# Two maps' query and key features side by side on the partitions, and their scores as pairs of 64-row products

## The chip, the cores and the metric

The kernel runs on one core of one Trainium2 chip. The metric is the device time of one execution in microseconds (us); three executions of the kernel before are shown, and their median is the time before.

## The reference

Two layers of a trunk over 512 latent tokens and 256 context tokens of width 1024. Each layer has a token-mixing part (a convolution branch and a differential attention, merged by gates) and an MLP. Only the attention is touched. It has 8 heads; each head has two softmax maps, and each map has its own queries and keys of 64 features:

```python
qb = q.reshape(B, nb, Q_BLOCK, N_HEADS, 2, QK_DIM).transpose(1, 0, 2, 3, 4, 5)
...
s = jnp.einsum('bqhcd,bkhcd->bhcqk', qi, keys, preferred_element_type=jnp.float32) * scale
p = jax.nn.softmax(s, axis=-1)
w = p[:, :, 0] - lam * p[:, :, 1]
return jnp.einsum('bhqk,bkhv->bqhv', w.astype(vals.dtype), vals)
```

Queries and keys are RMS-normalized over their 64 features, and those of latent tokens are rotated (rotary embedding) by cosine and sine tables. Latent queries read all 768 keys, context queries the 256 context keys. In the second layer only latent tokens have queries.

## The kernel before, in words

All values are float32. TensorE products run on float32r operands, and to keep the accuracy each operand is split into a high part (the value rounded to float32r, written by ScalarE) and a low part (the remainder, by VectorE or GpSimd). A full product takes three matmuls: high by high, high by low, low by high (`mm3`, lines 103 to 106).

Tokens lie in 6 tiles of 128 (tiles 0 to 3 latent, 4 and 5 context). Per layer, a loop over the heads `h` attends head `h` (`attend`) and, as filler between its steps, projects the next head (`qk_head`) and the next values (`v_pair`). `merge` deals the steps out by rough costs in us. That is only the order in which the program is written. The Tile framework's own scheduler then orders each engine's instructions by a simulated timeline, so that matmuls of several steps stand mixed on TensorE, and a product whose buffer comes free later is put later. The chip follows that order on each engine.

For head `h` and token tile `t`:

- `project(t)` makes queries and keys of both maps (tile `qk`, 128 tokens x 256), squares and sums them, and GpSimd takes the power -1/2 (L500). L501 multiplies. For latent tiles GpSimd makes the two rotary products `ra` and `rb` (L509, L513). Their sum is written twice into the tile `dup`, [128, 4, 2, 64], once by GpSimd and once by VectorE (L518), so that every 64 features stand twice side by side. Context tiles get the two copies by two GpSimd multiplications (L521).
- `turn(t, d)` turns `dup` by four TensorE transposes of 128x128 (L532, tile `qkT`, group 0 and 1 the queries of map 0 and 1, 2 and 3 the keys), so the features lie on the partitions, and each 64 features lie there twice, on partitions 0 to 63 and 64 to 127. ScalarE copies 128x512 to `QH` (L536), VectorE writes the queries' low parts `QL` (L537), and over the upper half of the keys their low parts (L539). So `QH[:, 2 + m]` holds the key's high part on 64 partitions and its low part on the other 64.
- `scores(t)` makes for each map `m` a PSUM tile `S` (pool `pS`, two buffers) of 128 queries x 768 keys, in a piece of 512 and one of 256 keys. One matmul over all 128 rows gives high query by high and low key at once (L660), a second adds the low query (L662). VectorE takes the row maximum of `S` (L664), ScalarE the exponential (L667), and that frees the buffer.
- The weights `e` are combined and turned (L690, tile `wT`), multiplied by the values (`av`), and normalized.

In the second layer the context tokens have keys only: `ctx_keys`, `ctx_norm` and `ctx_turn` project them, turn them, and turn them again in the doubled layout (L575, L579, L580).

The modulation of the next layer is computed beside the MLP by `ada_slab` (tile `adaps`): its matmuls (L216) have 32 columns of weights and address one of four column parts of the array by `tile_position=(0, 32 * j)`.

Of the kernel before, what the change touches and what calls it, by code (L numbers as in the profile page):

```python
# [8 lines left out]
F32 = mybir.dt.float32  # L9
F32R = mybir.dt.float32r  # L10
AF = mybir.ActivationFunctionType
# [3 lines left out]
P = 128  # L15
# [31 lines left out]
def f32(ap):  # L47
    return ap.bitcast(F32)
# [3 lines left out]
def trunk_kernel(  # L52
# [334 lines left out]
    for i in range(DEPTH):  # L387
# [90 lines left out]
        def qk_head(h):  # L478

            pre = first.pop("ps") if h == 0 else []  # L480
            w = first.pop("w") if h == 0 else qk_slab(i, h, both)
            QA = qp.tile([P, 4 * NT + 2 * nv], F32R, tag="qk", name=f"qk{i}_{h}")
            QH = QA[:, : 4 * NT].rearrange("p (g d) -> p g d", g=4)
            QL = QA[:, 4 * NT :].rearrange("p (g d) -> p g d", g=2)
            R = ap.tile([P, NTT, 4], F32, tag="rqk", name=f"rqk{i}_{h}")
            QKt[h] = QH, QL

            def project(t):
                given = t < len(pre)
                ps = pre[t] if given else mm_tile(f"qk{i}_{h}_{t}")  # L490
                for k in range(0 if given else KT):
                    mm3(ps[:, :256], hst(k, t), (w[0][:, k], w[1][:, k]), k == 0, k == KT - 1)
                rw = ap.tile([P, 4, QK], F32, tag="rw", name=f"rw{i}_{h}_{t}", bufs=4)
                nc.scalar.activation(out=rw, in_=ps[:, :256].rearrange("p (g d) -> p g d", g=4),
                                     func=AF.Copy)
                sq = sqs[next(turns) % 2]
                nc.scalar.activation(out=sq[:, :, :QK], in_=rw, func=AF.Square)
                r = R[:, t]
                nc.vector.tensor_reduce(out=r, in_=sq, axis=AX.X, op=ALU.add)
                nc.gpsimd.tensor_tensor(out=r, in0=r, in1=mhalf[:, :4], op=ALU.pow)  # L500
                (nc.gpsimd if last or t > 3 else nc.vector).tensor_tensor(  # L501
                    out=rw, in0=rw, in1=r.unsqueeze(2).to_broadcast([P, 4, QK]), op=ALU.mult)
                d = ap.tile([P, 4, 2, QK], F32, tag="dup", name=f"dup{i}_{h}_{t}", bufs=3)
                if t < 4:
                    a = ap.tile([P, 4, QK], F32, tag="sc", name=f"ra{i}_{h}_{t}", bufs=4)
                    b = ap.tile([P, 4, QK], F32, tag="sc", name=f"rb{i}_{h}_{t}", bufs=4)
                    v4 = rw.rearrange("p (s m) d -> p s m d", s=2)
                    bv = b.rearrange("p (s m) d -> p s m d", s=2)
                    nc.gpsimd.tensor_tensor(  # L509
                        out=a.rearrange("p (s m) d -> p s m d", s=2), in0=v4,  # L510
                        in1=L["tC"][:, t].unsqueeze(2).to_broadcast([P, 2, 2, QK]), op=ALU.mult)
                    for lo, o in ((0, hq), (hq, 0)):
                        nc.gpsimd.tensor_tensor(  # L513
                            out=bv[:, :, :, lo : lo + hq], in0=v4[:, :, :, o : o + hq],
                            in1=L["tS"][:, t, :, lo : lo + hq].unsqueeze(2)
                            .to_broadcast([P, 2, 2, hq]), op=ALU.mult)
                    for dup, eng in enumerate((nc.gpsimd, nc.vector)):
                        eng.tensor_tensor(out=d[:, :, dup], in0=a, in1=b, op=ALU.add)  # L518
                else:
                    for s in range(2):  # L520
                        nc.gpsimd.tensor_tensor(  # L521
                            out=d[:, 2 * s : 2 * s + 2],
                            in0=rw[:, 2 * s : 2 * s + 2].unsqueeze(2).to_broadcast([P, 2, 2, QK]),
                            in1=L["gr"][:, s].unsqueeze(1).unsqueeze(1)
                            .to_broadcast([P, 2, 2, QK]), op=ALU.mult)
                return d

            def turn(t, d):
                nm = f"qkT{i}_{h}_{t}"
                tp = turn_tile(nm) if turn_tile else mm_tile(nm)  # L530
                for g in range(4):
                    nc.tensor.transpose(tp[:, g * P : g * P + P],  # L532
                                        d[:, g].rearrange("p a d -> p (a d)"), ident)
                tpv = tp.rearrange("p (g d) -> p g d", g=4)
                ts = slice(t * P, t * P + P)
                nc.scalar.activation(out=QH[:, :, ts], in_=tpv, func=AF.Copy)  # L536
                nc.vector.tensor_tensor(out=QL[:, :, ts], in0=tpv[:, 0:2],  # L537
                                        in1=f32(QH[:, 0:2, ts]), op=ALU.subtract)
                nc.vector.tensor_tensor(out=QH[QK:, 2:4, ts], in0=tpv[QK:, 2:4],  # L539
                                        in1=f32(QH[QK:, 2:4, ts]), op=ALU.subtract)  # L540

            def ctx_keys():

# [7 lines left out]
            def ctx_norm(kc):  # L551
                tp = mm_tile(f"kcT{i}_{h}")
                for j in range(2):
                    nc.tensor.transpose(tp[:, j * P : j * P + P], kc[:, j * P : j * P + P], ident)
                rw = ap.tile([P, 4, QK], F32, tag="rw", name=f"rwc{i}_{h}", bufs=4)
                nc.scalar.activation(out=rw, in_=tp[:, :256].rearrange("p (g d) -> p g d", g=4),
                                     func=AF.Copy)
                sq = sqs[next(turns) % 2]
                nc.scalar.activation(out=sq[:, :, :QK], in_=rw, func=AF.Square)
                r = R[:, 4]  # L560
                nc.vector.tensor_reduce(out=r, in_=sq, axis=AX.X, op=ALU.add)
                nc.gpsimd.tensor_tensor(out=r, in0=r, in1=mhalf[:, :4], op=ALU.pow)
                nc.vector.tensor_tensor(out=rw, in0=rw, in1=r.unsqueeze(2).to_broadcast([P, 4, QK]),
                                        op=ALU.mult)
                d = ap.tile([P, 4, 2, QK], F32, tag="dup", name=f"dupc{i}_{h}", bufs=3)
                nc.gpsimd.tensor_tensor(
                    out=d, in0=rw.unsqueeze(2).to_broadcast([P, 4, 2, QK]),
                    in1=L["gr"][:, 1].unsqueeze(1).unsqueeze(1).to_broadcast([P, 4, 2, QK]),
                    op=ALU.mult)
                return d  # L570

            def ctx_turn(d):
                tp = mm_tile(f"kcD{i}_{h}")
                for g in range(4):
                    nc.tensor.transpose(tp[:, g * P : g * P + P],  # L575
                                        d[:, g].rearrange("p a d -> p (a d)"), ident)
                tpv = tp.rearrange("p (j m d) -> p m j d", j=2, m=2)
                o = QH[:, 2:4, CTXS].rearrange("p m (j d) -> p m j d", j=2)
                nc.scalar.activation(out=o, in_=tpv, func=AF.Copy)  # L579
                nc.vector.tensor_tensor(out=o[QK:], in0=tpv[QK:], in1=f32(o[QK:]),  # L580
                                        op=ALU.subtract)

            done = []
            for t in range(qt_n):
# [46 lines left out]
        def attend(h):  # L631
# [5 lines left out]
            def scores(t):  # L637
# [12 lines left out]
                ts = slice(t * P, t * P + P)  # L650
                es = []
                st = ap.tile([P, 8], F32, tag="st", name=f"st{nm}", bufs=4)
                for m in range(2):
                    S = pS.tile([P, 768], F32, tag="S", name=f"S{nm}_{m}")
                    for lo, hi in ((0, 512), (512, 768)):
                        lo = max(lo, kb * P)
                        if hi <= lo:
                            continue
                        o = slice(lo - kb * P, hi - kb * P)
                        nc.tensor.matmul(S[:, o], QH[:, m, ts], QH[:, 2 + m, lo:hi],  # L660
                                         start=True, stop=False)
                        nc.tensor.matmul(S[:, o], QL[:, m, ts], QH[:, 2 + m, lo:hi],  # L662
                                         start=False, stop=True)
                    nc.vector.tensor_reduce(out=st[:, m : m + 1], in_=S[:, :nkey], axis=AX.X,  # L664
                                            op=ALU.max, negate=True)
                    e = ap.tile([P, 768], F32, tag=f"e{m}", name=f"e{m}{nm}", bufs=2 - m)
                    nc.scalar.activation(out=e[:, :nkey], in_=S[:, :nkey], func=AF.Exp,  # L667
                                         bias=st[:, m : m + 1],
                                         accum_out=st[:, 2 + m : 3 + m])
                    es.append(e)  # L670
# [631 lines left out]
```

## Time and profile before

| | us |
|---|---|
| median of 3 executions | 2394.25 |
| lowest, highest | 2392.32, 2401.45 |
| the profiled execution | 2399.05 |
| its span in the trace | 2397.3 |
| TensorE busy with matmuls in it | 2317.9 (97%) |
| VectorE, ScalarE, GpSimd busy | 1349.1, 928.7, 679.7 |

In the rows of a profile, PE is TensorE's matmuls, PEld its weight loads, DVE VectorE, ACT ScalarE, POOL GpSimd and SP the queue that issues DMAs. A row names the line of the kernel, the operation, and the tile that is written, an arrow, and the tiles that are read. Attention lies at about 85 to 425 us (first layer) and 1481 to 1785 us (second layer). A matmul's shown length includes its way through the array, and the next one starts before it ends: how fast matmuls follow each other is read from their starts.

### The profile page before, as it was taken

The page shows a single profiled execution, that of the slowest core. Times are in us where ns is not written, and L with a number is a line of the kernel's source. Part 1 is how long each engine was busy: PE and PEld are TensorE (multiplying, and loading weights), DVE is VectorE, ACT ScalarE, POOL GpSimd, SP SyncE. Part 2 cuts the span into 40 slices and gives each one's busy share as a digit, 9 for nine tenths or more (in the row PEclk, how much of TensorE's full clock was granted, in tenths as well). Part 3 has the DMA queues.
Part 4 walks back from the last instruction along what each step waited for, and adds up shares of the span by engine and source line. Part 5 has one row for each costly group of instructions (what it writes and reads, how often), then busy time and mean ns, then how long its engine had stood idle before and what let it go on. Part 6 is the DMA issues. An engine that isn't in the chain of part 4 may idle for free.

```text
span 2397.3 us, 36929 instructions
## 1 busy us (share of the span) xinstructions
PE 2317.9 (97%) x15034; PEld 2060.9 (86%) x15034; DVE 1349.1 (56%) x2311; ACT 928.7 (39%) x1837; POOL 679.7 (28%) x854
## 2 busy tenths in 40 slices
PE   7999999999999999999999998999999989999998
PEld 6999998888888988888888997999877879888887
DVE  6777776699556542222222356676759966433332
ACT  5555654522333342221312345555642323422331
POOL 2866754200000222120211256676620000200110
PEclk9999999999999999999999999999999999999999
DMA  8211111144535223333333221111123324232322
GB/s 292 66 43 37 45 45 42 45 158 139 163 113 176 71 89 106 124 123 106 124 114 98 78 64 54 45 43 41 47 73 132 117 72 134 82 100 90 103 90 69
DMA packets 222186, 224.79 MB, mean 94 GB/s; under 512 B 5872, under 2 KB 212160, under 8 KB 221888
## 3 DMA queue, kind: packets, MB, share of 16 engines
q1 hardware_dynamic: 222016, 222.43, 28.9%
q8 instruction: 118, 1.93, 0.3%
q14 instruction: 52, 0.43, 0.1%
HBM read 208.73 MB, written 13.67 MB: 93 GB/s over the span
## 4 chain that ended last, share of the span: by engine, by line
PE 86%; DVE 7%; ACT 3%; POOL 2%; DMA 1%; issue 1%; SPq 0%; ACTq 0%; POOLq 0%; DVEq 0%
PE r L104 6%; PE r L106 6%; PE f L104 6%; PE r L105 6%; PE f L105 6%; PE f L106 6%; PE gt L104 3%; PE gt L106 3%; PE gt L105 3%; PE qk L104 3%; PE qk L105 2%; PE qk L106 2%; PE adaps L216 2%; PE v L104 2%; PE yc L113 2%; PE v L106 2%
## 5 line engine op out<-in xcount | busy, mean ns | idle before, releaser
L104 PE MATMUL r<-fh,h_w 128*128 128x512 f32 (+1 forms) x832 | 285.8, 345 | 0.5 <-DVE X L1082 0.5
L104 PE MATMUL f<-h2h,h_w 128*128 128x512 f32 (+1 forms) x832 | 284.6, 345 | 1.3 <-ACT h2h L76 1.0
L105 PE MATMUL f<-h2l,h_w 128*128 128x512 f32 (+1 forms) x832 | 284.5, 343 | 1.1 <-POOL h2l L77 1.0
L105 PE MATMUL r<-fl,h_w 128*128 128x512 f32 (+1 forms) x832 | 283.5, 341 | 0.0
L106 PE MATMUL r<-fh,l_w 128*128 128x512 f32 (+1 forms) x832 | 283.5, 341 | 0.0
L106 PE MATMUL f<-h2h,l_w 128*128 128x512 f32 (+1 forms) x832 | 282.6, 342 | 0.0
L76 ACT ACTIVATE h_w<-r_w 128x1024 fp32r<-128x1024 f32 x128 | 128.7, 1052 | 312.1 <-PE r L105 131.0
L1151 POOL TENSOR_TENSOR fr<-fr 128x512 f32<-128x512 f32 (+1 forms) x104 | 93.1, 897 | 508.7 <-ACT fh L1150 508.7
L897 DVE SCALAR_TENSOR_TENSOR cacc<-z,cols,cacc 128x783 f32<-128x783 f32 (+1 forms) x240 | 201.2, 890 | 0.3
L104 PE MATMUL qk<-h_wqk,h1h 128*128 128x256 f32 x640 | 183.9, 289 | 5.3 <-ACT h1h L76 3.6
L1082 DVE SCALAR_TENSOR_TENSOR X<-r,ad,X 128x512 f32<-128x512 f32 (+1 forms) x104 | 64.9, 627 | 209.8 <-PE r L106 209.7
L105 PE MATMUL qk<-l_wqk,h1h 128*128 128x256 f32 x640 | 181.2, 285 | 0.0
L104 PEld LDWEIGHTS f<-h2h,h_w 128*128 128x128 f32 x832 | 157.6, 191 | 24.8 <-ACT fh L1150 2.5
L104 PEld LDWEIGHTS r<-fh,h_w 128*128 128x128 f32 x832 | 157.8, 190 | 23.6 <-issue 3.7
L106 PE MATMUL qk<-h_wqk,h1l 128*128 128x256 f32 x640 | 177.6, 285 | 0.0
L105 PEld LDWEIGHTS f<-h2l,h_w 128*128 128x128 f32 x832 | 158.4, 191 | 20.5 <-POOL h2l L77 2.5
L106 PEld LDWEIGHTS f<-h2h,l_w 128*128 128x128 f32 x832 | 158.3, 191 | 17.6
L664 DVE TENSOR_REDUCE st<-S 128x1 f32<-128x768 f32 (+1 forms) x160 | 134.7, 846 | 68.4 <-PE S L662 67.4
L106 PEld LDWEIGHTS r<-fh,l_w 128*128 128x128 f32 x832 | 157.8, 190 | 17.8
L105 PEld LDWEIGHTS r<-fl,h_w 128*128 128x128 f32 x832 | 158.0, 190 | 16.9
L77 DVE TENSOR_TENSOR l_w<-r_w,h_w 128x1024 fp32r<-128x1024 f32 x106 | 126.2, 1223 | 80.5 <-ACT h_w L76 78.9
L1152 DVE TENSOR_TENSOR fl<-fr,fh 128x512 fp32r<-128x512 f32 (+1 forms) x104 | 62.5, 605 | 189.4 <-POOL fr L1151 189.3
(247 smaller groups left out, 6257.1 us busy)
## 6 DMA issues: line engine op xcount, KB each, us to landing
r_w<-in_w_mlp_dram SPq DMA_DIRECT2D x64, 1024.0 KB, 5.4
ada<-in_w_ada_dram SPq DMA_DIRECT2D x48, 1024.0 KB, 5.2
r_wqk<-in_w_in_dram SPq DMA_DIRECT2D x32, 512.0 KB, 5.2
r_wg<-in_w_in_dram SPq DMA_DIRECT2D x16, 1024.0 KB, 5.2
r_wv<-in_w_in_dram SPq DMA_DIRECT2D x8, 1024.0 KB, 5.2
r_wao<-in_w_attn_out_dram SPq DMA_DIRECT2D x8, 1024.0 KB, 5.2
r_wo<-in_w_out_dram SPq DMA_DIRECT2D x8, 1024.0 KB, 8.2
at_d<-uo SPq DMA_DIRECT2D x40, 128.0 KB, 1.7
```

The lines of the kernel that those rows point to most:

```text
L76: nc.scalar.activation(out=hi, in_=src, func=AF.Copy)
L77: (lo_eng or nc.vector).tensor_tensor(out=lo, in0=src, in1=f32(hi), op=ALU.subtract)
L104: nc.tensor.matmul(ps, sh, mh, start=first, stop=False)
L105: nc.tensor.matmul(ps, sh, ml, start=False, stop=False)
L106: nc.tensor.matmul(ps, sl, mh, start=False, stop=last)
L113: nc.tensor.matmul(ps, w[j][:, k, m0 : m0 + P], a(k)[0][:, toks], start=k + j == 0, stop=False)
L216: nc.tensor.matmul(ps[32 * j : 32 * j + 32, :256], cvec[:, k, :], r[:, k, :], start=k < 4, stop=k >= 4, tile_position=(0, 32 * j))
L664: nc.vector.tensor_reduce(out=st[:, m : m + 1], in_=S[:, :nkey], axis=AX.X, op=ALU.max, negate=True)
L897: nc.vector.scalar_tensor_tensor(out=ca[cc][:, :CV], in0=zt[cc][:, t : t + CV], scalar=wcol, in1=ca[cc][:, :CV], op0=ALU.mult, op1=ALU.add)
L1082: nc.vector.scalar_tensor_tensor(out=X[:, mb, g], in0=ps[:, :W], scalar=gate[:, s, mb : mb + 1], in1=X[:, mb, g], op0=ALU.mult, op1=ALU.add)
L1151: nc.gpsimd.tensor_tensor(out=r[:, :W], in0=r[:, :W], in1=r[:, :W], op=ALU.mult)
L1152: nc.vector.tensor_tensor(out=fl[mb][:, g], in0=r[:, :W], in1=f32(fh[mb][:, g]), op=ALU.subtract)
```

## The change

Queries and keys are no longer doubled. `dup` is [128, 4, 64]: the sum of the rotary products is made once, on VectorE, and context tiles take one multiplication. `turn` takes two transposes, one for the queries of both maps and one for the keys, so map 0 lies on partitions 0 to 63 and map 1 on 64 to 127. High and low part of queries and keys are written by `split`, 128x256 each (ScalarE copies, VectorE subtracts). `scores` makes both maps' `S` tiles first and then, for each piece of keys, three products per map over that map's 64 partitions: high by high, low query by high key, high query by low key. They are written in the order map 0, map 1, map 0, and so on. Each product has 64 rows, and the two maps use the two halves of the array's rows. An `S` tile is 1024 wide instead of 768.

```diff
-            QA = qp.tile([P, 4 * NT + 2 * nv], F32R, tag="qk", name=f"qk{i}_{h}")
-            QH = QA[:, : 4 * NT].rearrange("p (g d) -> p g d", g=4)
-            QL = QA[:, 4 * NT :].rearrange("p (g d) -> p g d", g=2)
+            QA = qp.tile([P, 4, NT], F32R, tag="qk", name=f"qk{i}_{h}")
+            QH, QL = QA[:, 0:2], QA[:, 2:4]
...
-                d = ap.tile([P, 4, 2, QK], F32, tag="dup", name=f"dup{i}_{h}_{t}", bufs=3)
+                d = ap.tile([P, 4, QK], F32, tag="dup", name=f"dup{i}_{h}_{t}", bufs=3)
...
-                    for dup, eng in enumerate((nc.gpsimd, nc.vector)):
-                        eng.tensor_tensor(out=d[:, :, dup], in0=a, in1=b, op=ALU.add)
+                    nc.vector.tensor_tensor(out=d, in0=a, in1=b, op=ALU.add)
                 else:
-                    for s in range(2):
-                        nc.gpsimd.tensor_tensor(
-                            out=d[:, 2 * s : 2 * s + 2],
...
+                    nc.gpsimd.tensor_tensor(
+                        out=d.rearrange("p (s m) d -> p s m d", s=2),
+                        in0=rw.rearrange("p (s m) d -> p s m d", s=2),
+                        in1=L["gr"].unsqueeze(2).to_broadcast([P, 2, 2, QK]), op=ALU.mult)
...
-                for g in range(4):
+                for g in range(2):
                     nc.tensor.transpose(tp[:, g * P : g * P + P],
-                                        d[:, g].rearrange("p a d -> p (a d)"), ident)
-                tpv = tp.rearrange("p (g d) -> p g d", g=4)
+                                        d[:, 2 * g : 2 * g + 2].rearrange("p m d -> p (m d)"),
+                                        ident)
+                tpv = tp[:, : 2 * P].rearrange("p (g d) -> p g d", g=2)
                 ts = slice(t * P, t * P + P)
-                nc.scalar.activation(out=QH[:, :, ts], in_=tpv, func=AF.Copy)
-                nc.vector.tensor_tensor(out=QL[:, :, ts], in0=tpv[:, 0:2],
-                                        in1=f32(QH[:, 0:2, ts]), op=ALU.subtract)
-                nc.vector.tensor_tensor(out=QH[QK:, 2:4, ts], in0=tpv[QK:, 2:4],
-                                        in1=f32(QH[QK:, 2:4, ts]), op=ALU.subtract)
+                split(QH[:, :, ts], QL[:, :, ts], tpv)
...
-                for m in range(2):
-                    S = pS.tile([P, 768], F32, tag="S", name=f"S{nm}_{m}")
-                    for lo, hi in ((0, 512), (512, 768)):
...
-                        nc.tensor.matmul(S[:, o], QH[:, m, ts], QH[:, 2 + m, lo:hi],
-                                         start=True, stop=False)
-                        nc.tensor.matmul(S[:, o], QL[:, m, ts], QH[:, 2 + m, lo:hi],
-                                         start=False, stop=True)
+                Ss = [pS.tile([P, 1024], F32, tag="S", name=f"S{nm}_{m}") for m in range(2)]
+                for lo, hi in ((0, 512), (512, 768)):
...
+                    for n, (a, b) in enumerate(((QH, QH), (QL, QH), (QH, QL))):
+                        for m, S in enumerate(Ss):
+                            pm = slice(m * QK, m * QK + QK)
+                            nc.tensor.matmul(S[:, o], a[pm, 0, ts], b[pm, 1, lo:hi],
+                                             start=n == 0, stop=n == 2)
+                for m, S in enumerate(Ss):
                     nc.vector.tensor_reduce(out=st[:, m : m + 1], in_=S[:, :nkey], axis=AX.X,
```

`ctx_norm` and `ctx_turn` change in the same way: one copy of the keys, two transposes instead of four, and `split`. The lines below `dup` shift: the transposes of `turn` are L529 afterwards, the scores L653, the turning of the weights L682.

The scheduler's order of TensorE changes with it. Layer 0, head 0, token tile 2, on TensorE: names are the tile, then layer, head, token tile and, for `S`, the map. Before, the end of map 1 of tile 1 and map 0 of tile 2 stood like this:

```order
L660 MATMUL S0_0_1_1_1167<-qk0_0_708 128x256
L662 MATMUL S0_0_1_1_1167<-qk0_0_708 128x256
L105 MATMUL qk0_1_3_1188<-l_wqk0_1_991,h1h_0_334 128x256
L106 MATMUL qk0_1_3_1188<-h_wqk0_1_990,h1l_0_335 128x256
L104 MATMUL qk0_1_3_1188<-h_wqk0_1_990,h1h_0_334 128x256
L105 MATMUL qk0_1_3_1188<-l_wqk0_1_991,h1h_0_334 128x256
L106 MATMUL qk0_1_3_1188<-h_wqk0_1_990,h1l_0_335 128x256
L660 MATMUL S0_0_2_0_1265<-qk0_0_708 128x512
L662 MATMUL S0_0_2_0_1265<-qk0_0_708 128x512
L660 MATMUL S0_0_2_0_1265<-qk0_0_708 128x256
L662 MATMUL S0_0_2_0_1265<-qk0_0_708 128x256
L532 MATMUL qkT0_1_1_1251<-cst_75,dup0_1_1_1076 128x128 x4
```

In the changed program the same tile's scores stand like this:

```order
L105 MATMUL qk0_1_4_1264<-l_wqk0_1_973,h1h_0_334 128x256
L106 MATMUL qk0_1_4_1264<-h_wqk0_1_972,h1l_0_335 128x256
L653 MATMUL S0_0_2_0_1239<-qk0_0_708 128x512 x3
L653 MATMUL S0_0_2_0_1239<-qk0_0_708 128x256 x3
L529 MATMUL qkT0_1_2_1321<-cst_75,dup0_1_2_1128 128x128 x2
L653 MATMUL S0_0_2_1_1240<-qk0_0_708 128x512 x3
L653 MATMUL S0_0_2_1_1240<-qk0_0_708 128x256 x3
L104 MATMUL qk0_1_5_1326<-h_wqk0_1_972,h1h_0_334 128x256
```

Four matmuls per map have become six, and all six of map 0 stand ahead of the six of map 1, with two transposes between them.

Layer 1, head 3, token tile 1, on TensorE. Before, map 0 stood like this, with map 1 some 70 instructions later:

```order
L660 MATMUL S1_3_1_0_16439<-qk1_3_15751 128x512
L662 MATMUL S1_3_1_0_16439<-qk1_3_15751 128x512
L660 MATMUL S1_3_1_0_16439<-qk1_3_15751 128x256
L662 MATMUL S1_3_1_0_16439<-qk1_3_15751 128x256
L104 MATMUL qk1_4_1_16331<-h_wqk1_4_16284,h1h_1_9374 128x256
```

In the changed program the end of the tile's scores stands like this:

```order
L106 MATMUL av1_2_1_16316<-wth1_2_1_1_15941,vl1_1_14963 128x256
L653 MATMUL S1_3_1_0_16384<-qk1_3_15701 128x512
L653 MATMUL S1_3_1_1_16385<-qk1_3_15701 128x512
L653 MATMUL S1_3_1_0_16384<-qk1_3_15701 128x256
L653 MATMUL S1_3_1_1_16385<-qk1_3_15701 128x256
L653 MATMUL S1_3_1_0_16384<-qk1_3_15701 128x256
L653 MATMUL S1_3_1_1_16385<-qk1_3_15701 128x256
L653 MATMUL S1_3_1_0_16384<-qk1_3_15701 128x256
L653 MATMUL S1_3_1_1_16385<-qk1_3_15701 128x256
L682 MATMUL wT1_3_0_0_16414<-cst_75,e01_3_0_16219 128x128
```

Here the maps alternate as the code is written. Counted over the whole program, 864 score matmuls stand in 185 unbroken stretches (114 in layer 0, 71 in layer 1), and between two stretches stand matmuls over 128 rows. In these stretches 105 pairs of neighbours are of different maps: 40 pairs of 512 keys, 54 of 256, 11 mixed. The other 654 matmuls have no partner of the other map beside them.

More of the change, by code (lines that the diff above doesn't have):

```diff
@@ L516, in project @@
                             .to_broadcast([P, 2, 2, hq]), op=ALU.mult)
-                    for dup, eng in enumerate((nc.gpsimd, nc.vector)):
-                        eng.tensor_tensor(out=d[:, :, dup], in0=a, in1=b, op=ALU.add)
-                else:
-                    for s in range(2):
-                        nc.gpsimd.tensor_tensor(
-                            out=d[:, 2 * s : 2 * s + 2],
-                            in0=rw[:, 2 * s : 2 * s + 2].unsqueeze(2).to_broadcast([P, 2, 2, QK]),
-                            in1=L["gr"][:, s].unsqueeze(1).unsqueeze(1)
-                            .to_broadcast([P, 2, 2, QK]), op=ALU.mult)
+                    nc.vector.tensor_tensor(out=d, in0=a, in1=b, op=ALU.add)
+                else:
+                    nc.gpsimd.tensor_tensor(
+                        out=d.rearrange("p (s m) d -> p s m d", s=2),
+                        in0=rw.rearrange("p (s m) d -> p s m d", s=2),
+                        in1=L["gr"].unsqueeze(2).to_broadcast([P, 2, 2, QK]), op=ALU.mult)
                 return d
@@ L564, in ctx_norm @@
                                         op=ALU.mult)
-                d = ap.tile([P, 4, 2, QK], F32, tag="dup", name=f"dupc{i}_{h}", bufs=3)
+                d = ap.tile([P, 4, QK], F32, tag="dup", name=f"dupc{i}_{h}", bufs=3)
                 nc.gpsimd.tensor_tensor(
-                    out=d, in0=rw.unsqueeze(2).to_broadcast([P, 4, 2, QK]),
-                    in1=L["gr"][:, 1].unsqueeze(1).unsqueeze(1).to_broadcast([P, 4, 2, QK]),
+                    out=d, in0=rw, in1=L["gr"][:, 1].unsqueeze(1).to_broadcast([P, 4, QK]),
                     op=ALU.mult)
@@ L573, in ctx_turn @@
                 tp = mm_tile(f"kcD{i}_{h}")
[L574 to L581, printed above, removed]
+                for j in range(2):
+                    nc.tensor.transpose(tp[:, j * P : j * P + P],
+                                        d[:, 2 * j : 2 * j + 2].rearrange("p m d -> p (m d)"),
+                                        ident)
+                split(QH[:, 1, CTXS], QL[:, 1, CTXS], tp[:, : 2 * P])
             done = []
@@ L652, in scores @@
                 st = ap.tile([P, 8], F32, tag="st", name=f"st{nm}", bufs=4)
-                for m in range(2):
-                    S = pS.tile([P, 768], F32, tag="S", name=f"S{nm}_{m}")
-                    for lo, hi in ((0, 512), (512, 768)):
[L656 to L660, printed above, removed]
-                                         start=True, stop=False)
-                        nc.tensor.matmul(S[:, o], QL[:, m, ts], QH[:, 2 + m, lo:hi],
-                                         start=False, stop=True)
+                Ss = [pS.tile([P, 1024], F32, tag="S", name=f"S{nm}_{m}") for m in range(2)]
+                for lo, hi in ((0, 512), (512, 768)):
+                    lo = max(lo, kb * P)
+                    if hi <= lo:
+                        continue
+                    o = slice(lo - kb * P, hi - kb * P)
+                    for n, (a, b) in enumerate(((QH, QH), (QL, QH), (QH, QL))):
[4 more added lines that the diff above has]
+                for m, S in enumerate(Ss):
                     nc.vector.tensor_reduce(out=st[:, m : m + 1], in_=S[:, :nkey], axis=AX.X,
```

## The prediction, made blind

> **What bounds the kernel now.** I read the page's busy shares and chain first, then the attention stages in the view by stretches, then the groups by shape, and last the order of time on TensorE.
>
> ```profile
> span 2397.3 us, 36929 instructions
> PE 2317.9 (97%) x15034; PEld 2060.9 (86%) x15034; DVE 1349.1 (56%) x2311; ACT 928.7 (39%) x1837; POOL 679.7 (28%) x854
> PE 86%; DVE 7%; ACT 3%; POOL 2%; DMA 1%; issue 1%; SPq 0%; ACTq 0%; POOLq 0%; DVEq 0%
> ```
>
> TensorE is busy 97% of the span and carries 86% of the chain. The next table has the two starts of a layer and the two attention stages; its second column is the length, the third TensorE's busy time.
>
> ```profile
> 48.00:85.00 37.00, 32.61 (x268) 31.85 (x269) 28.00 (x50) 18.10 (x37) 27.21 (x32) 1.00 0.29 98
> 85.00:425.00 340.00, 330.63 (x2558) 317.67 (x2557) 249.01 (x506) 196.09 (x492) 215.09 (x315) 0.98 0.14 43
> 1445.00:1481.00 36.00, 29.98 (x217) 27.74 (x216) 22.74 (x38) 21.96 (x42) 26.25 (x32) 0.95 0.20 60
> 1481.00:1785.00 304.00, 290.20 (x2140) 274.13 (x2139) 205.49 (x359) 163.27 (x370) 173.64 (x241) 0.98 0.16 49
> ```
>
> TensorE stands idle 4.4 + 9.4 + 6.0 + 13.8 = 33.6 us in these four stretches together. So in the stages that the change touches, what TensorE gains or loses is the time, and shorter work elsewhere can return 33.6 us at the very most. What a matmul costs there is the distance of the starts:
>
> ```profile
> 200.64 0.40 PE L662 MATMUL S<-qk 128*128 128x512 f32 x1
> 200.87 0.28 PE L660 MATMUL S<-qk 128*128 128x256 f32 x1
> 200.99 0.28 PE L662 MATMUL S<-qk 128*128 128x256 f32 x1
> 201.11 0.28 PE L105 MATMUL qk<-l_wqk,h1h 128*128 128x256 f32 x1
> ...
> 202.17 0.60 PE L532 MATMUL qkT<-cst,dup 128*128 128x128 f32 x4
> 202.52 0.36 PE L104 MATMUL v<-h_wv,h1h 128*128 128x256 f32 x1
> 202.73 0.28 PE L105 MATMUL v<-l_wv,h1h 128*128 128x256 f32 x1
> ```
>
> A score matmul of 512 keys takes 0.23 us (200.64 to 200.87), one of 256 keys 0.12 (200.87 to 200.99). Four transposes and the first matmul behind them take 202.17 to 202.73 = 0.56 us; less that matmul's 0.12 it is 0.44, or 0.11 for one transpose.
>
> **The change, part by part.** The counts:
>
> ```profile
> L660 PE MATMUL S<-qk 128*128 128x512 f32 x128 | 55.5, 434 | 4.2 <-ACT e L667 4.2
> L662 PE MATMUL S<-qk 128*128 128x512 f32 x128 | 51.1, 399 | 0.0
> L660 PE MATMUL S<-qk 128*128 128x256 f32 x160 | 46.8, 294 | 2.5 <-ACT e L667 2.5
> L662 PE MATMUL S<-qk 128*128 128x256 f32 x160 | 45.5, 286 | 0.0
> L532 PE MATMUL qkT<-cst,dup 128*128 128x128 f32 x320 | 50.0, 276 | 6.6 <-DVE qk L539 2.1 <-POOL dup L518 2.1 <-POOL dup L521 1.9
> ```
>
> (1) *Third product, if nothing overlaps.* Before, two matmuls per piece: 256 x 0.23 + 320 x 0.12 = 58.9 + 38.4 = 97.3 us. Three per piece, each over 64 rows with as many columns to stream: 145.9. That is +48.6 us.
>
> (2) *Pairs that do overlap.* Two matmuls can share the array only when they are neighbours in TensorE's order and belong to different maps. The changed order has 105 such pairs among 864 matmuls, and this decides the case: in layer 0 nearly every map's matmuls stand alone. That disjoint parts of the array do work at once this trace shows, for columns:
>
> ```profile
> 857.26 0.28 PE L105 MATMUL f<-h2l,h_w 128*128 128x256 f32 x1
> 857.38 0.28 PE L106 MATMUL f<-h2h,l_w 128*128 128x256 f32 x1
> 857.59 0.62 PE L216 MATMUL adaps<-ada,cvec 128*32 128x256 f32 x2
> 858.14 0.38 PE L104 MATMUL f<-h2h,h_w 128*128 128x256 f32 x1
> 858.45 1.07 PE L216 MATMUL adaps<-ada,cvec 128*32 128x256 f32 x16
> 859.45 0.39 PE L105 MATMUL f<-h2l,h_w 128*128 128x256 f32 x1
> 859.67 0.28 PE L106 MATMUL f<-h2h,l_w 128*128 128x256 f32 x1
> 859.79 0.28 PE L104 MATMUL f<-h2h,h_w 128*128 128x256 f32 x1
> 860.00 0.63 PE L216 MATMUL adaps<-ada,cvec 128*32 128x256 f32 x6
> 860.56 0.39 PE L105 MATMUL f<-h2l,h_w 128*128 128x256 f32 x1
> ```
>
> Six matmuls in three column parts take 0.56 us (860.00 to 860.56), two in one part 0.55 (857.59 to 858.14). For row halves no row exists. If a pair costs one matmul, laying the 185 stretches out with 0.23 and 0.12 saves 17 us; if the two weight loads of a pair follow each other at 0.107 us, it saves 9. The load's time comes from these two rows, (191 - 110) ns for 96 columns, times 128/96:
>
> ```profile
> L660 PEld LDWEIGHTS S<-qk 128*128 128x128 f32 x288 | 54.9, 191 | 14.3 <-ACT e L667 8.4 <-ACT osq L705 0.4
> L216 PEld LDWEIGHTS adaps<-ada,cvec 128*32 128x32 f32 x768 | 21.1, 110 | 16.9 <-issue 1.8 <-PE ya L106 0.8 <-PE ya L104 0.3
> ```
>
> I take the middle, -13 us.
>
> (3) *Visits to the 64-row shape.* The 864 matmuls form 185 stretches, each between matmuls over 128 rows. What a change of the array's shape costs is bounded by the column shape above. Entry: 857.38 to 857.59 is 0.21 where 0.12 is usual, +0.09. Exit: 859.45 to 859.67, +0.10. Inside, one part does 2 matmuls in 0.55 us and the full group does 4 per part in 1.00, so a matmul takes 0.225 and 0.10 is left over. Together 0.29 us a visit. The lower end is 0 (row halves need no pause), the upper 0.37: a score's weight load is 0.08 us longer than the one of 32 columns (191 against 110 ns) and may lie open at the entry. I take 0.29, the only measured change of shape: 185 x 0.29 = +54 us; ends 0 and +68. On this the Trainium skill has a rule (TensorEngine Tiling (Array Packing), Key Properties): another tiling mode, though not another tile of the same mode, drains TensorE. By it the 185 visits pay and the sum is the one below; without it the first rival holds. The trace agrees with it for columns (0.29 us); nothing here shows it for rows.
>
> (4) *Transposes.* 80 turns lose two each, and 8 context turns in layer 1 too: 176 x 0.11 = -19.4 us, all on TensorE's path.
>
> (5) *Work taken from the other engines.*
>
> ```profile
> L539 DVE TENSOR_TENSOR qk<-qkT,qk 64x256 fp32r<-64x256 f32 x80 | 34.2, 427 | 1.1
> L518 POOL TENSOR_TENSOR dup<-ra,rb 128x256 f32<-128x256 f32 x64 | 53.7, 841 | 1.9
> L521 POOL TENSOR_TENSOR dup<-rw,gr 128x256 f32<-128x256 f32 x32 | 26.9, 862 | 1.1
> L536 ACT ACTIVATE qk<-qkT 128x512 fp32r<-128x512 f32 x80 | 47.8, 600 | 15.5 <-PE qkT L532 15.1
> L494 ACT ACTIVATE rw<-qk 128x256 f32<-128x256 f32 x80 | 30.2, 385 | 61.1 <-PE qk L106 52.7 <-POOL rb L513 4.3 <-POOL rqk L500 2.5
> ```
>
> VectorE loses L539, 34.2 us; GpSimd 53.7 and half of 26.9; ScalarE copies 256 columns instead of 512, 600 to about 385 ns, 80 x 0.215 = 17 us. Together about 118 us of engine time, but TensorE's matmuls cover it. It is worth only the idle time that ends with these operations. TensorE's own longer work also lets late producers catch up, in the same gaps. I take a third of 33.6, -12 us; ends 0 and -33.6. What stays late is the exponential that frees a score buffer, 6.7 us (L660, above): the first matmul of each map waits for it as before, and everything behind it on TensorE waits too. No DMA is moved or resized.
>
> Sum: 48.6 - 13 + 54 - 19.4 - 12 = +58 us. The profiled execution took 2399.05 (2397.3 span), 5 us above the median of 2394.25; added to the median it is **2452 us**. With the bounds of the other terms and a visit between 0.19 (entry and exit alone) and 0.37 it reaches from 48.6 - 17 + 35 - 19.4 - 33.6 = +14 to 48.6 - 9 + 68 - 19.4 = +88, 2408 to 2482.
>
> **The rivals.** *A: the visit is free.* If a matmul over 64 rows may follow one over 128 without a pause, the sum is 48.6 - 13 - 19.4 - 12 = +4: 2398 us, no change that can be told (0.5%, 12 us, is about what a measurement of this kernel can tell). With the bounds of (2) and (5) it is -21 to +20, 2373 to 2414. For it speaks that row halves, unlike columns, keep all 128 output columns and the same full weight load. Against it speaks the only change of shape that the trace has. It decides below 0.04 us a visit (4 + 185 x 0.043 = 12).
>
> *B: an unhidden weight load.* Successive matmuls of one map use the same half. If the next load must wait for the matmul in flight, 512 such successions pay 0.107 us, +55 us: 2507 us. The Trainium skill says so (TensorE: Matmul & The Clock Gate, The mechanism): a weight load overlaps a running matmul only when their row groups differ. Against it: before, all score matmuls use the same 128 rows and still follow at 0.12 us with a load of 0.107 in each, so the load is hidden. On that evidence the rule gets a small chance.
>
> *C: the pairs overlap after all*, as the code is written. All 432 pairs at one matmul each: 73 us instead of 97.3, -24; with the transposes and the gaps -55 without visits, 2339 us; with visits about 2393. For it speaks that six column matmuls take as long as two (above). It would need partners to overlap with other matmuls between them, and the changed order parts 654 of the 864 from any partner; that nearly excludes it.
>
> **How the numbers follow.** My sum 0.66, A 0.18, B 0.08, C 0.03, and 0.05 for what I have not seen. The range from 2392 to 2495 holds nearly all of the first, two thirds of A and a little of the rest, near 0.8. The likeliest case alone: 2408 to 2482. Faster by over 0.5% needs the low end of A or C: 0.06. Within 0.5% is most of A and part of C: 0.14. Slower: 0.80.
>
> **What the profile after would show.** (1) Score matmuls x384 of 512 keys and x480 of 256, all with 64 rows, and lone ones still 0.23 and 0.12 us apart; 0.33 and 0.22 would be B. (2) Neighbours of different maps starting almost together, but only about 105 times, most of them in layer 1. (3) The first score behind a `qk` or `v` matmul about 0.2 us behind it, and a like step at the exit; 0.12 us there is A. (4) 176 transposes fewer. (5) L539 gone, TensorE's idle in the two stages some 12 us less. Layer 0's attention stage should grow more than layer 1's, as it has 114 of the visits and few of the pairs. A stage that grows less than TensorE's own sum would mean that I underrated the gaps; one that shrinks, that a pair saves more than a matmul.

## The result, and the profile after

The changed kernel takes 2447.6 us (median of 4 executions, 2442.69 to 2453.99) against 2393.55 before: ratio 1.0222, 95% interval 1.0203 to 1.024. It is 54 us slower; 58 were forecast. The profiled execution took 2442.69 us, the lowest of the four, 43.6 us more than the profiled one of before. The page's first lines, as shown of before:

```profile
span 2440.9 us, 36884 instructions
PE 2377.4 (97%) x15146; PEld 2066.4 (85%) x15146; DVE 1300.1 (53%) x2231; ACT 911.3 (37%) x1837; POOL 600.4 (25%) x774
PE 91%; DVE 4%; ACT 2%; DMA 1%; issue 1%; POOL 1%; ACTq 0%; SPq 0%; DVEq 0%; POOLq 0%
```

VectorE is relieved by 49 us, ScalarE by 17, GpSimd by 79. TensorE carries 91% of the chain instead of 86%. Where the time went is read from three marks in TensorE's order of time: the first gate matmul (`gt`) after the first layer's attention, the last MLP matmul of the first layer (`r`), and the first gate matmul of the second layer. Before:

```profile
477.88 0.28 PE L104 MATMUL gt<-h1h,h_wg 128*128 128x256 f32 x1
1410.84 0.28 PE L106 MATMUL r<-fh,l_w 128*128 128x256 f32 x1
1815.71 0.78 PE L104 MATMUL gt<-h1h,h_wg 128*128 128x512 f32 x1
```

After:

```profile
520.00 0.28 PE L104 MATMUL gt<-h1h,h_wg 128*128 128x256 f32 x1
1447.70 0.28 PE L106 MATMUL r<-fh,l_w 128*128 128x256 f32 x1
1859.82 0.78 PE L104 MATMUL gt<-h1h,h_wg 128*128 128x512 f32 x1
```

The first attention takes 520.00 - 477.88 = 42 us more, the second (1859.82 - 1447.70) - (1815.71 - 1410.84) = 7 us more, and the first layer's remainder 5 us less. The score matmuls and the transposes in the groups by shape:

```profile
L653 PE MATMUL S<-qk 64*128 64x512 f32 x384 | 111.7, 435 | 0.7 <-ACT e L659 0.6
L653 PE MATMUL S<-qk 64*128 64x256 f32 x480 | 80.8, 294 | 1.7 <-ACT e L659 1.5
L529 PE MATMUL qkT<-cst,dup 128*128 128x128 f32 x160 | 31.6, 279 | 2.8 <-DVE qk L77 1.2 <-DVE dup L517 0.8 <-ACT rwc L550 0.8
```

The order of time shows what a visit to the 64-row shape costs. It names a stretch by its first form; that the first one holds three matmuls of 256 keys of one map, the second six of alternating maps, and the third twelve, 512 keys and then 256, alternating, comes from the program's order.

```profile
128.34 0.28 PE L104 MATMUL qk<-h_wqk,h1h 128*128 128x256 f32 x1
128.55 0.61 PE L653 MATMUL S<-qk 64*128 64x256 f32 x3
129.09 0.39 PE L105 MATMUL qk<-l_wqk,h1h 128*128 128x256 f32 x1
...
1498.28 0.28 PE L106 MATMUL qk<-h_wqk,h1l 128*128 128x256 f32 x1
1498.49 0.62 PE L653 MATMUL S<-qk 64*128 64x256 f32 x6
1499.04 0.39 PE L104 MATMUL qk<-h_wqk,h1h 128*128 128x256 f32 x1
1499.26 0.28 PE L105 MATMUL qk<-l_wqk,h1h 128*128 128x256 f32 x1
...
1592.98 1.31 PE L653 MATMUL S<-qk 64*128 64x512 f32 x12
1594.22 0.44 PE L682 MATMUL wT<-cst,e 128*128 128x128 f32 x2
```

The entry is 0.21 us where 0.12 is usual (128.34 to 128.55), and so is the step behind the stretch (1499.04 to 1499.26, 0.22). Three lone matmuls of 256 take 0.54 us, 0.18 more than 3 x 0.12; over all 185 stretches it is about 0.20. So a visit costs 0.09 + 0.20 + 0.10 = 0.39 us. Six alternating matmuls take 0.55 us, as long as three of one map: a pair costs one matmul. Twelve alternating ones take 1.24 (1592.98 to 1594.22).

The 185 stretches sum to 162.4 us from their starts to the next matmul's; with 0.19 at the ends of each they cost 197.5 us, where 97.3 stood before.

### The profile page after: what moved, and what is told of

It is laid out like the page before. It is cut to its first block, busy times and chain, and to the rows that moved or that the text cites. A ratio compares the mean times of both kernels' runs of the same rounds, so it can differ in the third digit from the quotient of the medians.

```text
span 2440.9 us, 36884 instructions
## 1 busy us (share of the span) xinstructions
PE 2377.4 (97%) x15146; PEld 2066.4 (85%) x15146; DVE 1300.1 (53%) x2231; ACT 911.3 (37%) x1837; POOL 600.4 (25%) x774
## 4 chain that ended last, share of the span: by engine, by line
PE 91%; DVE 4%; ACT 2%; DMA 1%; issue 1%; POOL 1%; ACTq 0%; SPq 0%; DVEq 0%; POOLq 0%
PE r L104 6%; PE S L653 6%; PE r L106 6%; PE r L105 6%; PE f L104 6%; PE f L105 6%; PE f L106 6%; PE qk L104 3%; PE qk L105 3%; PE qk L106 3%; PE gt L104 3%; PE gt L106 3%; PE gt L105 3%; PE adaps L216 2%; PE wT L682 2%; PE v L104 2%
## 5 line engine op out<-in xcount | busy, mean ns | idle before, releaser
L653 PE MATMUL S<-qk 64*128 64x512 f32 (+1 forms) x864 | 174.4, 357 | 2.3 <-ACT e L659 2.1
L105 PEld LDWEIGHTS r<-fl,h_w 128*128 128x128 f32 x832 | 157.8, 190 | 16.8
```

The costliest lines, as they stand in the source:

```text
L105: nc.tensor.matmul(ps, sh, ml, start=False, stop=False)
L653: nc.tensor.matmul(S[:, o], a[pm, 0, ts], b[pm, 1, lo:hi], start=n == 0, stop=n == 2)
```

## The experiments

**A visit by itself.** `visit1` is the kernel before, with half the rows of one matmul left out in each block of the first MLP product, where TensorE runs with few gaps:

```diff
-                fm_block(ps[:, :W], w, m * P, lambda k: (h2h[:, k], h2l[:, k]), g)
+                for k in range(KT):
...
+                    n_ = QK if k == 4 else P
+                    nc.tensor.matmul(ps[:, :W], wl[:n_], ah_[:n_], start=False, stop=k == KT - 1)
```

> The kernel before, with one change in the first MLP product: in each of its 104 blocks of 24 matmuls the low-weight matmul of the fifth k is made over 64 rows only (it leaves out half of that one product), at the same number of columns. TensorE runs without gaps there, so the price of a visit to the 64-row shape stands alone. Theory 1 (a visit costs 0.39 us, as read from the changed kernel's trace): +41 us, ratio 1.017. The price taken in the prediction (0.29): +30 us, 1.0125. Rival (no cost by itself; the score stretches of the changed kernel are slow because of their own buffers): under +5 us.

Measured: 2430.94 us, ratio 1.0148 (1.0132 to 1.0164), so 35 us (32 to 39). `visit2` makes the matmul ahead of it over 64 rows too (shown against `visit1`):

```diff
-                    nc.tensor.matmul(ps[:, :W], wh, al_, start=False, stop=False)
+                    nc.tensor.matmul(ps[:, :W], wh[:n_], al_[:n_], start=False, stop=False)
```

> As the run before it, but in each block two successive matmuls (low hidden and low weight of the fifth k) are made over the same 64 rows, so about as many visits with twice the 64-row matmuls; half of two products is left out. Theory 1 (the cost is the change of shape, once per visit): +41 us again, 1.017. Rival (each 64-row matmul or its weight load costs, whatever stands beside it): +81 us, 1.034.

Measured: 2436.9 us, ratio 1.0174 (1.0156 to 1.0191), 42 us (37 to 46). Twice the 64-row matmuls do not double the cost, so it belongs to the change of shape. The order of time of `visit1` and then of `visit2`:

```profile
902.51 0.39 PE L1151 MATMUL f<-h2l,h_w 128*128 128x512 f32 x1
902.83 0.50 PE L1153 MATMUL f<-h2h,l_w 64*128 64x512 f32 x1
903.26 0.50 PE L1150 MATMUL f<-h2h,h_w 128*128 128x512 f32 x1
903.60 0.39 PE L1151 MATMUL f<-h2l,h_w 128*128 128x512 f32 x1
```

```profile
901.25 0.49 PE L1152 MATMUL f<-h2l,h_w 64*128 64x512 f32 x1
901.58 0.39 PE L1153 MATMUL f<-h2h,l_w 64*128 64x512 f32 x1
901.91 0.50 PE L1150 MATMUL f<-h2h,h_w 128*128 128x512 f32 x1
902.24 0.40 PE L1152 MATMUL f<-h2l,h_w 128*128 128x512 f32 x1
```

With one 64-row matmul the steps are 0.32, 0.43 and 0.34 where 0.23 is usual, together 0.40 us more; with two, 901.25 to 902.24 is 0.99 for three steps, 0.30 more, and the entry ahead of them adds 0.09. Both are 0.39 to 0.40. For 104 visits that is 41 us, and summed over all of them the two traces have 41 us (`visit1`) and 43 (`visit2`). `visit2` took that much longer; `visit1` took some 6 us less than its visits add up to, for which nothing shows the cause.

**Pairs and fewer visits.** `one_tile` is the changed kernel with both maps' scores in one PSUM tile, so that the scheduler finds all twelve products ready at once:

```diff
-                Ss = [pS.tile([P, 1024], F32, tag="S", name=f"S{nm}_{m}") for m in range(2)]
+                SS = pS.tile([P, 2, 1024], F32, tag="S", name=f"S{nm}", bufs=1)
+                Ss = [SS[:, m] for m in range(2)]
```

> The changed kernel, but both maps' scores lie in one PSUM tile with one buffer, so all twelve products of a token tile become ready together. The order then has 108 visits instead of 185, and nearly every matmul stands in a pair. Theory 1 (visit 0.39, a pair costs one matmul, gaps as in the changed kernel): scores 72 + 108 x 0.39 = 114 us instead of 96 before, transposes -19, gaps -38: -43 us, near 2352, ratio 0.983. Rival (with one buffer TensorE waits for both maps' exponentials before the next tile's scores): the gaps come back, 2395 to 2420, ratio 1.00 to 1.01. Rival (pairs held up by their weight loads): 8 us more than theory 1.

Measured: 2386.92 us, 0.9968 (0.9956 to 0.998). It is faster than both kernels, but neither the 2352 of theory 1 nor the rival's 2395 to 2420 came: TensorE's own work came out as expected (its score stretches sum to 118 us with their ends, 114 expected), and the gaps did not stay as small as in the changed kernel (the table below).

`mapwise` has the same tile and nearly the same visits, but writes the products of map 0 ahead of those of map 1:

```diff
-                    for n, (a, b) in enumerate(((QH, QH), (QL, QH), (QH, QL))):
-                        for m, S in enumerate(Ss):
+                for m, S in enumerate(Ss):
...
+                        for n, (a, b) in enumerate(((QH, QH), (QL, QH), (QH, QL))):
```

> The one-tile kernel (one PSUM tile for both maps, 108 visits) with the twelve products written map by map instead of alternating: six of map 0, then six of map 1; 107 visits, the same work. Theory 3 (the two row halves run side by side as far as TensorE looks ahead, a few matmuls: 1.81 us for such a stretch in the changed kernel's trace against 1.24 alternating): about 47 stretches x 0.57 = +27 us over the one-tile kernel on TensorE, of which the gaps take a third: 2403 to 2414 us, 1.004 to 1.009. Rival (only neighbours overlap): +49 us on TensorE, 2418 to 2436. Rival (the order within a stretch does not matter): 2387.

Measured: 2417.65 us, 1.0103 (1.0087 to 1.0118), 31 us slower than `one_tile` by the order of the same matmuls alone, 4 us above theory 3's span and just under the first rival's 2418. The trace decides between them: it has 47 stretches of twelve, nearly all of 1.8 us:

```profile
138.29 1.90 PE L654 MATMUL S<-qk 64*128 64x512 f32 x12
140.12 0.38 PE L105 MATMUL qk<-l_wqk,h1h 128*128 128x256 f32 x1
```

One after the other the twelve would take 6 x 0.23 + 6 x 0.12 + 0.20 = 2.3 us, and side by side 1.24. So the second map's matmuls start while some of the first map's still stand ahead of them, but not when six do. Both rivals are out: with only neighbours overlapping, 2.3 us would stand in place of 1.8, and if the order did not matter, 1.24.

**The gaps.** `relief` is the kernel before, without most of the work that the change takes from VectorE and GpSimd:

```diff
-                    for dup, eng in enumerate((nc.gpsimd, nc.vector)):
-                        eng.tensor_tensor(out=d[:, :, dup], in0=a, in1=b, op=ALU.add)
+                    nc.vector.tensor_tensor(out=d, in0=a, in1=b, op=ALU.add)
...
-                                        d[:, g].rearrange("p a d -> p (a d)"), ident)
+                                        d[:, g // 2 * 2 : g // 2 * 2 + 2].rearrange("p m d -> p (m d)"),
+                                        ident)
...
-                nc.vector.tensor_tensor(out=QH[QK:, 2:4, ts], in0=tpv[QK:, 2:4],
-                                        in1=f32(QH[QK:, 2:4, ts]), op=ALU.subtract)
```

> The kernel before with TensorE's work as it was (four transposes, two 128-row products) but with most of the work that the change takes from the other engines taken away: the second copy of the sums (GpSimd), the second multiplication of the context tiles, and the low part over the keys' upper half (VectorE). The low parts of the keys are left out, and the transposes read the two maps side by side twice, so the scores are not those of the reference. Theory 2 (the gaps of TensorE close because the other engines have less to do): -20 to -35 us, near 2365, 0.988. Rival (they close because TensorE takes longer and the others catch up): 0 to -6 us, 0.998 to 1.000.

Measured: 2394.55 us, 0.9997 (0.9984 to 1.001): no gain. `wb_pool` goes the other way, the changed kernel with GpSimd's work put back (the latent tiles are shown; context tiles get a second multiplication in the same way):

```diff
                     nc.vector.tensor_tensor(out=d, in0=a, in1=b, op=ALU.add)
+                    x = ap.tile([P, 4, QK], F32, tag="xtra", name=f"xt{i}_{h}_{t}", bufs=1)
+                    nc.gpsimd.tensor_tensor(out=x, in0=a, in1=b, op=ALU.add)
...
```

> The changed kernel with GpSimd's removed work put back as a copy that nobody reads: a second sum of the rotary products per latent tile and a second multiplication per context tile, about 67 us of GpSimd time, at their old place. 181 visits instead of 185. Theory 2b: as the changed kernel, 2442 to 2452 us, ratio 1.020 to 1.024. Theory 2 (relief): +10 to +25 us over it, 1.027 to 1.034.

Measured: 2449.78 us, 1.0233 (1.0219 to 1.0247), which holds the changed kernel's 1.0222. The page's busy shares, of `relief` and then of `wb_pool`, show that the work did move:

```profile
PE 2310.6 (97%) x15034; PEld 2057.0 (86%) x15034; DVE 1310.7 (55%) x2231; ACT 926.4 (39%) x1837; POOL 611.1 (26%) x774
```

```profile
PE 2379.9 (97%) x15146; PEld 2069.5 (85%) x15146; DVE 1309.0 (54%) x2231; ACT 911.2 (37%) x1837; POOL 670.1 (27%) x854
```

69 us less on GpSimd than before bought no time, and 70 us more than in the changed kernel cost none that can be told. `third128` gives TensorE more work and takes nothing from the others:

```diff
-                        nc.tensor.matmul(S[:, o], QL[:, m, ts], QH[:, 2 + m, lo:hi],
-                                         start=False, stop=True)
+                        for n in range(2):
+                            nc.tensor.matmul(S[:, o], QL[:, m, ts], QH[:, 2 + m, lo:hi],
+                                             start=False, stop=n == 1)
```

> The kernel before with its second score product (low query) made twice, so three 128-row products per piece; nothing else is touched, the order on TensorE is nearly that of before, and the low query counts double in the scores. TensorE gets 128 x 0.23 + 160 x 0.12 = 48.6 us more, the other engines nothing less. Theory 2b (TensorE's gaps in the attention close because it takes longer while the others work on): +25 to +36 us, ratio 1.010 to 1.015. Theory 2 (the gaps closed only because the others had less to do): +46 to +50 us, 1.019 to 1.021.

Measured: 2424.22 us, 1.0125 (1.0112 to 1.0139): 30 us for 48.6 us of work. So theory 2 falls, and theory 2b holds: 18 us of gaps closed with nothing taken from the other engines. The table puts the eight traces side by side over both attention stages (from 62 us to the first gate matmul, and from the last `r` to the next gate matmul). TensorE's own work is its counts by the distances of undisturbed starts (0.227 for 512 columns, 0.119 for 256, 0.11 for a transpose, 0.09 for a column sum), with 64-row stretches as their traces have them plus 0.19 each; the rest is what is left of the length.

| kernel | length | TensorE's own work | rest |
|---|---|---|---|
| `one_low` (below) | 810 | 739 | 71 |
| before | 821 | 740 | 80 |
| `relief` | 821 | 741 | 79 |
| `one_tile` | 811 | 744 | 68 |
| `mapwise` | 840 | 782 | 59 |
| `third128` | 844 | 788 | 56 |
| changed kernel | 870 | 823 | 47 |
| `wb_pool` | 873 | 825 | 48 |

From 740 to 823 us of work the rest falls from 80 to 47: about 0.4 us of gap closes for each us that TensorE gets more to do. These are single executions; by the medians it is 0.37 for `third128` (18 of 48.6) and 0.33 for the changed kernel (27 of 81). `one_tile` and `one_low` do not fit: TensorE has as much to do in them as before, and their rest is 68 and 71 instead of 80. Nothing shows what closed those gaps.

**A better version.** `one_low` is `one_tile` with the products that need low parts first:

```diff
-                    for n, (a, b) in enumerate(((QH, QH), (QL, QH), (QH, QL))):
+                    for n, (a, b) in enumerate(((QH, QL), (QL, QH), (QH, QH))):
```

> The one-tile kernel with the products that need the low parts written first, so that a stretch starts only when all its operands are there: 97 visits instead of 108. By 0.39 us a visit -4 us against the one-tile kernel on TensorE, of which part goes to gaps: 2383 to 2387 us, 0.9955 to 0.997. If later starts of the scores cost more than the visits, 2390 or more.

Measured: 2382.54 us, 0.9958 (0.9945 to 0.9971), 11 us faster than before and 65 faster than the changed kernel. The gain over `one_tile` (2386.92) lies within the intervals of the two. A full stretch in its order of time:

```profile
115.18 1.31 PE L654 MATMUL S<-qk 64*128 64x512 f32 x12
116.43 0.39 PE L105 MATMUL v<-l_wv,h1h 128*128 128x256 f32 x1
```

1.25 us for twelve matmuls: with the ends 1.44 us, against 1.40 for the eight of 128 rows (4 x 0.23 + 4 x 0.12). The scores are no cheaper than before even when every pair overlaps. All 97 stretches with their ends sum to 112 us, 15 more than before; less the transposes' 19.4 us that is only some 4 us less work for TensorE (1 in the table). The rest of the 11 us came out of the gaps, and as in `one_tile` the cause of that stays open.

## Why the prediction was right, step by step

The forecast (2452, measured 2447.6) and its main mechanism hold: the scheduler parts the pairs, and the visits to the 64-row shape cost more than the transposes give back. Three sizes were off: the visits cost 18 us more than forecast, the pairs saved 8 more and the gaps 15 more (against the medians). These cancel to 5 us, so the closeness of the forecast is partly luck.

(1) *Third product.* Right: lone 64-row matmuls cost what 128-row ones do. In the 56 stretches of three of 512 and three of 256 keys of one map it is 1.24 us, that is 3 x 0.23 + 3 x 0.12 + 0.20:

```profile
95.83 1.31 PE L653 MATMUL S<-qk 64*128 64x512 f32 x6
97.07 0.33 PE L529 MATMUL qkT<-cst,dup 128*128 128x128 f32 x1
```

(2) *Pairs.* -13 was taken, -21 came (145.9 + 185 x 0.39 - 197.5). A pair costs one matmul, the better end of the bounds: two weight loads do not hold it up. And the step's premise, that only neighbours overlap, was wrong: three matmuls of one map followed by three of the other took 0.55 us, as three alone, and `mapwise` lost only about half of the overlap. In the changed kernel's order of time (which map a matmul belongs to comes from the program's order), three and three of 256 keys, two and two of 512 (0.66 us), and three and three of each length for one map after the other (1.81 us):

```profile
498.87 0.62 PE L653 MATMUL S<-qk 64*128 64x256 f32 x6
499.42 0.55 PE L682 MATMUL wT<-cst,e 128*128 128x128 f32 x3
...
1799.30 0.73 PE L653 MATMUL S<-qk 64*128 64x512 f32 x4
1799.96 0.39 PE L104 MATMUL av<-wth,vh 128*128 128x256 f32 x1
...
203.93 1.88 PE L653 MATMUL S<-qk 64*128 64x512 f32 x12
205.74 0.39 PE L104 MATMUL qk<-h_wqk,h1h 128*128 128x256 f32 x1
```

(3) *Visits.* The step that was too small: 0.29 us taken from the column shape, 0.39 measured, outside the upper end of 0.37. The entry (0.09) and the exit (0.10) were right, and the 0.10 inside is 0.20. That is +72 us instead of +54. The Trainium skill's rule cited there (TensorEngine Tiling (Array Packing), Key Properties) fits the trace for rows too: alternating between the halves costs nothing within a stretch (0.55 us for six), leaving the shape 0.39. That the 0.39 us is a drain, no run shows.

(4) *Transposes.* Right: 160 are left of 320 in `turn`, at unchanged distances (0.11 x 176).

(5) *Gaps.* The step with the wrong size, and only one of its two reasons held. A third of the 33.6 us of visible idle was to return, -12 us, because the other engines get less to do and because TensorE's own longer work lets them catch up. Between the profiled executions the sum 48.6 - 20.6 + 72.2 - 19.4 = +81 met +43.6, so 37 us returned; against the medians, 27. TensorE's own extra time closes gaps (`third128`). That less work on VectorE and GpSimd does, `relief` and `wb_pool` do not show; ScalarE's 17 us were not tried alone. A sign that the prediction named came: both stages grew less than TensorE's own sum (by 42 and 7 us, where its work grew by 57 and 26). Visible idle over the table's stretches fell from 820.75 - 776.36 = 44.4 us to 870.12 - 841.00 = 29.1, before and after:

```profile
sum 820.75, PE 776.36 PEld 733.82 DVE 577.66 ACT 450.71 POOL 485.13; mean PE 388.18 PEld 366.91 DVE 288.83 ACT 225.36 POOL 242.57
sum 870.12, PE 841.00 PEld 744.33 DVE 529.97 ACT 434.73 POOL 404.99; mean PE 420.50 PEld 372.16 DVE 264.99 ACT 217.37 POOL 202.49
```

These 15 us are not all that returned, since visible idle isn't all that a gap costs. Behind the gap in the next rows TensorE ran at a lower clock. Before, in the view by stretches (the last three columns are granted clock, DMA share and GB/s):

```profile
385.00:390.00 5.00, 2.10 (x10) 1.22 (x8) 4.92 (x8) 3.21 (x7) 2.27 (x3) 0.92 0.05 6
390.00:395.00 5.00, 4.57 (x19) 4.22 (x19) 3.63 (x8) 1.37 (x3) 4.00 (x6) 0.50 0.63 209
```

After, at the same time:

```profile
385.00:390.00 5.00, 5.00 (x41) 4.73 (x40) 3.38 (x6) 3.12 (x6) 0.00 (x1) 1.00 0.02 5
390.00:395.00 5.00, 5.00 (x38) 4.59 (x37) 2.63 (x6) 0.82 (x3) 2.60 (x4) 1.00 0.65 210
```

2.9 us of idle are followed by 5 us at half the clock, 19 matmuls where an undisturbed stretch holds 38. That the idle time brings the lower clock is read from this order of events; no run forces it. Summed over stretches of 5 us from 40 us on, 5 x (1 - clock) is 28.9 us before and 16.8 after: of the 37 us about 12 are clock. Most of these 12 are chance: the profiled execution of before had a granted clock of 0.988, that of the changed kernel 0.993, the highest of its four. Over all executions the means are 0.989 and 0.991, so that about 5 of the 27 us are clock.

The rivals: A needed a visit under 0.04 us, and it is 0.39. B is out, since successive matmuls of one half keep their distance: six of one map take 0.20 us more than their streaming (95.83 to 97.07, above), where five waits for a load would add 0.54. The Trainium skill's rule beside it (TensorE: Matmul & The Clock Gate, The mechanism) does not hold here: by that stretch the loads are hidden though all six use the same rows. C is out for the changed kernel. What it describes is `one_tile`, where the pairs do overlap, but with its 108 visits the scores cost 118 us there, against 97 before. As forecast, the first layer grew by far the more, with 114 of the visits and few alternating stretches.

## What to carry to other kernels

Small-row products in pairs pay only if they stay together: count, in the order that the scheduler really made, how often the array changes shape, and price each visit (0.39 us here) like three matmuls of 256 columns. Give the products a common buffer, so that they become ready together, and write the partners alternately. And where TensorE is close to full but has gaps, as in this attention, added work on it came through at 0.6 to 0.7 of its size (30 us of 48.6, 54 of 81), while work taken from VectorE and GpSimd came through at nothing. In the MLP, which has few gaps, nearly all of it came through (35 and 42 us for visits of 41 and 43).

## What the runs showed of the hardware that I had not expected

The two row halves run ahead of each other: two matmuls of 512 keys of one map and then two of the other took 0.66 us, as two alone do, without alternating; behind six of the other half the overlap falls to about half (1.81 us against 1.24 and 2.3). Two weight loads in one pair cost nothing: twelve matmuls with twelve loads took 1.24 us, six with six the same. A change of shape by rows costs 0.39 us, 0.10 more than the prediction read for columns, and whatever the number of 64-row matmuls in it (one, two or six).
